# Storing the first of eleven tiles of a row softmax through ScalarE's DMA queue instead of GpSimd's

## The chip, the cores and the metric

The kernel runs on one core of a Trainium2 chip. The core has five engines, each with an instruction stream of its own. Four matter here: VectorE (DVE in the profile), ScalarE (ACT), GpSimd (POOL) and SyncE (SP). Three of them issue transfers: SP all loads, POOL and ACT the stores. The transfers of each issuer form one queue (in the profile's tables q1 is SP's, q0 is POOL's and q10 is ACT's), and all queues are worked off by the same 16 DMA engines. The metric is device time in microseconds (us). The kernel before takes 317.07 us, the median of three runs that lie between 317.07 and 317.11 us.

## What is computed

A softmax over the last axis of a float32 array of 32 x 512 x 1024, with a temperature of 0.5:

```python
scaled = x / temperature
shifted = scaled - np.max(scaled, axis=-1, keepdims=True)
exp_x = np.exp(shifted)
return exp_x / np.sum(exp_x, axis=-1, keepdims=True)
```

That is 16,384 rows of 1024 elements: 67.11 MB are read and 67.11 MB written.

## The kernel before

The rows are cut into eleven tiles (`PASSES`): the first ten hold 12 rows on each of the 128 partitions (6144 KB a tile), the last holds 8 (4096 KB). A tile is worked on in place, in groups of rows: tile 0 in three groups of 4, tiles 1 to 9 in two groups of 6, tile 10 in two groups of 4. There are 23 groups. In what follows, L0 to L10 are the loads of the tiles and S0 to S10 their stores.

Four buffers hold tiles (`BUFS = 4`). A tile is loaded into a buffer by SP (line 60), and the load of tile i+4 waits until the store of tile i has landed, since it takes that buffer. The first four loads are issued at once.

For each group DVE takes the maximum of each row (line 69) and scales it to a bias (line 72); ACT computes the exponentials row by row, with their sum (line 78); DVE takes the reciprocals of the sums (line 90) and multiplies, either all rows in one instruction (line 93, tiles in `WHOLE`) or row by row (line 96). After a tile's last group it is stored (line 108).

The order is written out by hand. For a group g the program emits maximum(g) and exponential(g), and then divide(g-1) and, where g-1 ends a tile, store(g-1) and the load of a further tile. From tile 9 on (`ALONE`), a tile's first group is emitted after the divide and store of the group before it. Each engine runs its own part in that order. So a store issued by ACT stands in ACT's stream behind the exponentials of the group after the tile: S0, if issued by ACT, comes behind the 12 exponentials of tile 0 and the 6 of tile 1's first group, and ahead of the 6 of tile 1's second group.

S0 to S5 are issued by POOL, S6 to S10 by ACT (`BY_POOL = 6`). Ahead of S0, POOL copies one column of tile 2 into a small tile named `seen` (line 106): POOL's stream waits there until L2 has landed. The multiplication of tile 2's first group waits for that copy too, because it overwrites what the copy reads.

Of the kernel before, what the change touches and what calls it, by code (L numbers as in the profile page):

```python
# [1 line left out]

# [4 lines left out]

PASSES = [[4, 4, 4]] + [[6, 6]] * 9 + [[4, 4]]  # L10
BUFS = 4

WHOLE = (2, 3, 4, 6, 8)


BY_POOL = 6

ALONE = 9


@with_exitstack
def kernel(
    ctx: ExitStack,
    tc: tile.TileContext,
    x: bass.AP,
    temperature: bass.AP,
    out: bass.AP,
):
    nc = tc.nc
    f32 = mybir.dt.float32  # L30
    scale = 1.0 / float(temperature)
    extreme = mybir.AluOpType.max if scale > 0 else mybir.AluOpType.min

    P = 128
    xf = x.flatten_outer_dims()
    of = out.flatten_outer_dims()
    n, d = xf.shape
    rows = [sum(ks) for ks in PASSES]
    assert sum(rows) * P == n

    data = ctx.enter_context(tc.tile_pool(name="data", bufs=BUFS))
    stats = ctx.enter_context(tc.tile_pool(name="stats", bufs=4))


    groups = []
    for i, ks in enumerate(PASSES):
        for j, k in enumerate(ks):
            groups.append((i, sum(ks[:j]), k))

    def dram(t, i):  # L50
        block = t[P * sum(rows[:i]) : P * sum(rows[: i + 1]), :]
        return block.rearrange("(p k) d -> p k d", p=P, k=rows[i])

    tiles, small = [], []

    def load():
        i = len(tiles)
        if i < len(PASSES):
            xt = data.tile([P, rows[i], d], f32, name="xt")
            nc.sync.dma_start(out=xt, in_=dram(xf, i))  # L60
            tiles.append(xt)

    def maximum(g):
        i, a, k = groups[g]
        top, bias, sums, recip = (
            stats.tile([P, k], f32, name=name) for name in ("top", "bias", "sums", "recip")
        )
        small.append((bias, sums, recip))
        nc.vector.tensor_reduce(  # L69
            out=top, in_=tiles[i][:, a : a + k, :], axis=mybir.AxisListType.X, op=extreme  # L70
        )
        nc.vector.tensor_scalar_mul(bias, in0=top, scalar1=-scale)  # L72

    def exponential(g):
        i, a, k = groups[g]
        bias, sums, _ = small[g]
        for b in range(k):
            nc.scalar.activation(  # L78
                tiles[i][:, a + b, :],
                tiles[i][:, a + b, :],  # L80
                mybir.ActivationFunctionType.Exp,
                bias=bias[:, b : b + 1],
                scale=scale,
                accum_out=sums[:, b : b + 1],
            )

    def divide(g):
        i, a, k = groups[g]
        _, sums, recip = small[g]
        nc.vector.reciprocal(recip, sums)  # L90
        if i in WHOLE:
            xt = tiles[i][:, a : a + k, :]
            nc.vector.tensor_mul(xt, xt, recip.unsqueeze(2).to_broadcast([P, k, d]))  # L93
            return
        for b in range(k):
            nc.vector.tensor_scalar_mul(  # L96
                tiles[i][:, a + b, :], in0=tiles[i][:, a + b, :], scalar1=recip[:, b : b + 1]
            )

    def store(g):  # L100
        i, a, k = groups[g]
        if a + k == rows[i]:
            if i == 0:


                nc.gpsimd.tensor_copy(stats.tile([P, 1], f32, name="seen"), tiles[2][:, 0, 0:1])  # L106
            queue = nc.gpsimd if i < BY_POOL else nc.scalar
            queue.dma_start(out=dram(of, i), in_=tiles[i])  # L108
            load()

    with tc.manual_schedule():
        for _ in range(BUFS):
            load()
        for g in range(len(groups) + 1):

            alone = g < len(groups) and groups[g][0] >= ALONE and groups[g][1] == 0
            if g > 0 and alone:
                divide(g - 1)  # L120
                store(g - 1)
            if g < len(groups):
                maximum(g)
                exponential(g)
            if g > 0 and not alone:
                divide(g - 1)
                store(g - 1)


# [1 line left out]
_INS = ['x', 'temperature']  # L131
_OUTS = [((32, 512, 1024), 'float32')]

_NUMBERS = {'temperature': 0.5}


# [26 lines left out]
```

## Time and profile before

The profiled execution has a span of 315.8 us from its first to its last instruction; the runs' median is 317.07 us, 1.3 us more.

| | us |
|---|---|
| median of the runs | 317.07 |
| span of the profiled execution | 315.8 |
| DVE busy | 256.9 (81%) |
| ACT busy | 148.3 (47%) |
| POOL busy | 3.7 (1%) |

The DMA engines move 134.24 MB in the span, a mean of 425 GB/s. The trace gives for each transfer its issue and the time to its landing. Worked out as issue plus time to landing:

| tile | load issued | landed | store issued (by) | landed |
|---|---|---|---|---|
| 0 | 0.74 | 18.2 | 47.89 (POOL) | 77.1 |
| 4 | 77.20 | 110.9 | 153.74 (POOL) | 190.3 |
| 5 | 103.10 | 139.7 | 179.94 (POOL) | 221.1 |
| 6 | 132.31 | 168.7 | 211.22 (ACT) | 246.5 |
| 7 | 161.31 | 197.7 | 239.51 (ACT) | 272.5 |
| 8 | 190.44 | 228.5 | 259.97 (ACT) | 290.7 |
| 9 | 221.25 | 257.5 | 284.63 (ACT) | 305.2 |
| 10 | 246.68 | 281.6 | 301.35 (ACT) | 314.9 |

S1, S2 and S3 are issued by POOL at 69.47, 96.49 and 124.95 us and land at 103.1, 132.2 and 161.2 us.

In the page's table of slices each digit is the busy share of a fortieth of the span, in tenths; 9 is 90% or more. In a timeline row the columns are the start, the duration, the engine (ACTq, POOLq, SPq: the sequencer, which issues and waits), the line, the operation, what it writes and reads, the count and, in brackets, the idle time before it with what ended that.

### The profile page before, as it was taken

To read this page: it belongs to the slowest core of one execution; us is meant where nothing else is said; L and a number is where in the kernel's file an instruction comes from. 1 tells how busy PE (TensorE), PEld (TensorE's weight loads), DVE (VectorE), ACT (ScalarE), POOL (GpSimd) and SP (SyncE) were. 2 spreads that over 40 slices of the span, in tenths; PEclk is the share of its full clock that TensorE was granted. 3 is DMA by queue.
4 is the path that set the end of the run, shared out by engine and by line. 5 is a ranking of instruction groups with operands and counts; after the bars stand their busy time and mean duration, and the time that the engine had idled before them with its cause. 6 is when DMAs were issued, how large, how long until landed. Compare 5 with 4: busy or idle time off the path is not lost.

```text
span 315.8 us, 525 instructions
## 1 busy us (share of the span) xinstructions
DVE 256.9 (81%) x147; ACT 148.3 (47%) x257; POOL 3.7 (1%) x11
## 2 busy tenths in 40 slices
DVE  0069999999999899979976994999199999969710
ACT  0029636775461807344471744074416802953700
POOL 0000001000000000000000000000000000000000
DMA  8999999999999999999999999999999999999996
GB/s 305 473 417 423 461 411 399 399 468 430 400 479 417 417 461 411 430 467 405 442 448 399 455 442 405 467 424 417 461 417 430 455 401 463 411 452 411 455 411 270
DMA packets 3171, 134.24 MB, mean 425 GB/s; under 512 B 352, under 2 KB 352, under 8 KB 352
## 3 DMA queue, kind: packets, MB, share of 16 engines
q1 hardware_dynamic: 1584, 67.11, 49.7%
q0 software_dynamic: 864, 37.75, 27.6%
q10 hardware_dynamic: 720, 29.36, 21.5%
q14 instruction: 3, 0.02, 0.0%
HBM read 67.11 MB, written 67.11 MB: 425 GB/s over the span
## 4 chain that ended last, share of the span: by engine, by line
DMA 47%; DVE 28%; ACT 11%; issue 9%; DVEq 0%; SPq 0%; POOLq 0%
DMA xt<-in_x_dram 25%; DMA out_dram<-xt 22%; DVE top L69 16%; ACT xt L78 11%; DVE xt L96 8%; DVE xt L93 2%; DVE bias L72 0%; DVE recip L90 0%; DVEq L158 0%; SPq L60 0%; POOLq L108 0%
## 5 line engine op out<-in xcount | busy, mean ns | idle before, releaser
L78 ACT ACTIVATE xt<-xt,bias 128x1024 f32<-128x1024 f32 x128 | 145.2, 1135 | 131.7 <-DVE recip L90 70.6
L69 DVE TENSOR_REDUCE top<-xt 128x6 f32<-128x6144 f32 (+1 forms) x23 | 139.9, 6083 | 37.8 <-DMA xt<-in_x_dram 37.8
L93 DVE TENSOR_TENSOR xt<-xt,recip 128x6144 f32<-128x6144 f32 x10 | 65.6, 6558 | 0.4
L96 DVE TENSOR_SCALAR xt<-xt,recip 128x1024 f32<-128x1024 f32 x68 | 46.2, 749 | 0.5
L78 ACT ACTIVATION_READ_ACCUMULATOR xt<-xt,bias 128x1 f32 x128 | 23.9, 187 | 0.0
L78 ACT ACT_TABLE_LOAD x1 | 1.3, 1283 | 18.3 <-DMA xt<-in_x_dram 18.3
L90 DVE RECIPROCAL recip<-sums 128x6 f32<-128x6 f32 (+1 forms) x23 | 4.2, 182 | 5.0 <-ACT xt L78 5.0
L108 POOL DMA_DIRECT2D out_dram<-xt x6 | 3.3, 554 | 129.6 <-ACT xt L78 82.7
L72 DVE TENSOR_SCALAR bias<-top 128x6 f32<-128x6 f32 (+1 forms) x23 | 3.9, 171 | 0.8
L106 POOL COPY seen<-xt 128x1 f32<-128x1 f32 x1 | 0.2, 185 | 46.9 <-DMA xt<-in_x_dram 46.9
L144 POOL MEMSET const-uint8-127<- 128x1 uint8 x1 | 0.1, 103 | 0.0
L144 POOL MEMSET const-bfloat16-1.0<- 128x1 bf16 x1 | 0.1, 102 | 0.0
L144 POOL MEMSET const-float32-0.0<- 128x1 f32 x1 | 0.1, 99 | 0.2 <-issue 0.2
L144 POOL MEMSET const-float32-1.0<- 128x1 f32 x1 | 0.1, 98 | 0.0
## 6 DMA issues: line engine op xcount, KB each, us to landing
xt<-in_x_dram SPq DMA_DIRECT2D x10, 6144.0 KB, 36.4
out_dram<-xt POOLq DMA_DIRECT2D x6, 6144.0 KB, 35.9
out_dram<-xt ACTq DMA_DIRECT2D x4, 6144.0 KB, 31.9
xt<-in_x_dram SPq DMA_DIRECT2D x1, 4096.0 KB, 34.9
out_dram<-xt ACTq DMA_DIRECT2D x1, 4096.0 KB, 13.5
```

The source lines that it names most:

```text
L69: nc.vector.tensor_reduce(out=top, in_=tiles[i][:, a : a + k, :], axis=mybir.AxisListType.X, op=extreme)
L72: nc.vector.tensor_scalar_mul(bias, in0=top, scalar1=-scale)
L78: nc.scalar.activation(tiles[i][:, a + b, :], tiles[i][:, a + b, :], mybir.ActivationFunctionType.Exp, bias=bias[:, b : b + 1], scale=scal ...
L90: nc.vector.reciprocal(recip, sums)
L93: nc.vector.tensor_mul(xt, xt, recip.unsqueeze(2).to_broadcast([P, k, d]))
L96: nc.vector.tensor_scalar_mul(tiles[i][:, a + b, :], in0=tiles[i][:, a + b, :], scalar1=recip[:, b : b + 1])
L106: nc.gpsimd.tensor_copy(stats.tile([P, 1], f32, name="seen"), tiles[2][:, 0, 0:1])
L108: queue.dma_start(out=dram(of, i), in_=tiles[i])
L144: nc = _bacc.Bacc("TRN2", target_bir_lowering=False, num_devices=1)
```

## The change

S0 is issued by ACT. S1 to S5 stay with POOL and S6 to S10 with ACT. The copy into `seen` stays in POOL's stream, now ahead of S1. Nothing else in the program is different: the arithmetic, the tiles, the buffers and the order of the groups are the same.

```diff
                 nc.gpsimd.tensor_copy(stats.tile([P, 1], f32, name="seen"), tiles[2][:, 0, 0:1])
-            queue = nc.gpsimd if i < BY_POOL else nc.scalar
+            queue = nc.gpsimd if 0 < i < BY_POOL else nc.scalar
             queue.dma_start(out=dram(of, i), in_=tiles[i])
             load()
```

In the built program ACT's stream gains one transfer, which waits for DVE alone, and POOL's loses one. SP's loads stand in the same order; the load of tile 4 still waits for S0's landing.

## The prediction

> **What bounds the kernel now.** I read the slices of the whole span first, then the DMA view in stretches, then the issues of the stores one by one, and last the chain of waits for the tail.
>
> ```profile
> span 315.8 us, 525 instructions
> DMA  8999999999999999999999999999999999999996
> HBM read 67.11 MB, written 67.11 MB: 425 GB/s over the span
> ```
>
> The DMA engines are busy in every slice but the first and the last. The DMA view of four stretches (20 to 49, 49 to 60, 60 to 280 and 305 to 316 us):
>
> ```profile
> DMA packets 288, 12.58 MB, mean 434 GB/s; under 512 B 32, under 2 KB 32, under 8 KB 32
> ...
> DMA packets 88, 4.33 MB, mean 393 GB/s; under 512 B 0, under 2 KB 0, under 8 KB 0
> ...
> DMA packets 2235, 95.45 MB, mean 434 GB/s; under 512 B 248, under 2 KB 248, under 8 KB 248
> ...
> DMA packets 118, 3.34 MB, mean 304 GB/s; under 512 B 16, under 2 KB 16, under 8 KB 16
> ```
>
> Loads alone (20 to 49) go at 434 GB/s. So does the stretch from 60 to 280, in which loads mix with stores of POOL and then of ACT. So 434 GB/s is what this core's engines give, whatever the mix and whoever issued. At that rate 134.24 MB take 309.3 us; 6.5 us of the span are something else:
> - start: the stretch 0 to 20 moves 7.86 MB, which is 18.1 us of work: 1.9 us lost;
> - 49 to 60, where S0 joins L3: 4.33 MB are 10.0 us of work in 11: **1.0 us lost**, the only dip between the ends;
> - 305 to 316: 3.34 MB are 7.7 us of work in 10.8: 3.1 us lost, of which 0.9 lie behind the last landing (301.35 + 13.5 = 314.85) and 2.2 are engines that finish unevenly.
>
> Together 6.0, with 0.5 of rounding at the edges of the stretches. So the kernel is bound by DMA throughput; the compute matters only where it would leave the queues empty. The timeline around S0 and around ACT's first store of now (S6):
>
> ```profile
> 47.31 0.18 POOL L106 COPY seen<-xt 128x1 f32<-128x1 f32 x1 [46.86 <-DMA xt<-in_x_dram]
> 47.35 6.55 DVE L69 TENSOR_REDUCE top<-xt 128x6 f32<-128x6144 f32 x1
> 47.89 0.67 POOL L108 DMA_DIRECT2D out_dram<-xt  x1 [0.40 <-DVE xt L96]
> ...
> 50.29 1.13 ACT L78 ACTIVATE xt<-xt,bias 128x1024 f32<-128x1024 f32 x1
> ...
> 54.20 1.15 ACT L78 ACTIVATE xt<-xt,bias 128x1024 f32<-128x1024 f32 x1 [2.68 <-DVE recip L90]
> ...
> 69.47 0.53 POOL L108 DMA_DIRECT2D out_dram<-xt  x1 [20.91 <-DVE xt L96]
> ...
> 210.21 1.13 ACT L78 ACTIVATE xt<-xt,bias 128x1024 f32<-128x1024 f32 x1
> 211.22 0.97 ACTq L108 DMA_DIRECT2D out_dram<-xt  x1
> ...
> 301.35 0.34 ACTq L108 DMA_DIRECT2D out_dram<-xt  x1
> ```
>
> To be seen here: the copy into `seen` holds S0 back by nothing, since the multiplications of tile 0 end with the start of the maximum at 47.35; POOL has 20.91 us of idle time ahead of S1; and ACT idles 2.68 us ahead of its work at 54.20.
>
> **The change part by part.**
>
> *S0 leaves POOL.* Removed: one issue of 0.67 us on an engine that is 1% busy: 0 us, hidden by POOL's 20.91 us of idle time. S1 waits for DVE until 69.17 in any case, and the copy ahead of it is over at 47.5: S1 to S5 keep their times.
>
> *S0 stands in ACT's stream.* ACT runs in order, so S0 waits for the exponentials of tile 1's first group. S6 was issued 1.01 us after the start of the last exponential ahead of it (210.21 to 211.22); the same behind 50.29 gives 51.30. S0 is issued **3.4 us later** than at 47.89. Its wait for DVE (47.4) is long over. The issue takes between 0.34 us (ACT's later ones, 301.35) and 0.97 us (its first, S6); S0 is now the first, so I take 0.97, to 52.3. What is queued behind it is the exponential of 54.20, which waits for DVE's bias anyway: 1.9 us to spare, cost 0. Without that cover, ACT would be late by 0.97 us at most, and DVE's reciprocal behind it by as much. S6's issue becomes a later one and shrinks by 0.6 us; its cover is the 6.40 us that ACT idles behind it: 0.
>
> *S0 and S1 lie on two queues.* Before, S1 stood behind S0 on POOL's queue. Now they can run side by side from about 70 us. The nearest row is S5, whose last 10 us ran beside S6 from ACT's queue: 41.2 us to landing, against 36.6 for S4, so 4.6 longer. L8, in flight at the same time, took 38.1 against the 36.4 of L6 and L7. For S0 that is an upper bound, since L3 loses nothing by S0's later start and gets out of the way sooner. S0 would land between 77.1 + 3.4 = 80.5 and 80.5 + 4.6 = 85.1. I take 81, nearest to the lower end: S1's first turns come only when S0 has a quarter left. L4 waits for this landing, is issued 3.4 to 8 us later and lands by about 3.5 us later (114 for 110.9). DVE, which waits 1.67 us for L4 now, waits about 5.
>
> The Trainium skill's page "DMA: Bandwidth & Descriptors", section "Queues, rings and completion order", speaks against the change here: each DMA engine takes turns between the queue rows that have work, a packet at a time, so a second row for stores takes turns from whatever is in flight. By the rule alone, what S0 has left when S1 begins (some 8 us: 80.5 less 72) would take twice as long and L4 be issued near 88.5 instead of 77.2; carried whole to the tail that would be some 10 us. By the row of S5 it is 8 us at most, and the next step says why I carry none of it.
>
> *Where that stall goes.* Nothing is lost as long as some queue has work. Late next is L4 by 3.5 us; but the engines' turns that L4 doesn't take are taken by S1, which lands some 4 us sooner than 103.1, and L5 is issued then, behind L4. From there a load is always waiting: before, L5 is issued at 103.1 and L4 lands at 110.9, and each pair after that overlaps by 7 us. A later L4 makes these overlaps longer. The stores, ahead by as much, run dry once for some microseconds around S6, and there the loads catch up. Work done in another order: 0 us.
>
> *The tail.* The chain from L8's landing (228.5) through DVE and ACT to S10's issue (301.35) has no DMA wait in it. S10 lands 13.5 us after its issue, since S9 lands only at 305.2 and 4.19 MB take 9.7 us at 434 GB/s. L0, with 14.5 us of data, landed 17.5 after its issue, so a lone S10 would need 9.7 + 3.0 = 12.7: the chain has **0.8 us of slack**. I take L8 as not later than now, since S5 and S6 overlap less; cost 0.
>
> *The dip of 1.0 us at S0.* The trace of before shows that it comes with the first store; it doesn't show whether with the first write at all, with the first use of POOL's queue, or with that queue joining loads. When ACT's queue is first used (S6, 212 to 222) the rate is 452 GB/s, no dip. With the first write, it stays, at S0; with POOL's first use, it moves to S1. Bounds: -1.0 (it goes) to +1.0 (one at S0 and another at S1). I take 0, which two of the readings give.
>
> Sum: 0 + 0 + 0 + 0 + 0. Span 315.8, and with the 1.3 us around it **317.1 us**, the median of the runs. The uneven finish of the engines (2.2 us) can shift by some tenths either way, so the forecast's own range is 316.5 to 317.7.
>
> **The rivals.**
> - *The dip goes* (28%). For it: ACT's first use showed none, and when POOL's queue is now first used, at 69.5, L3 may have landed, so no load is there to be held up. Against: the first packets of the program are slow too, so a first use may cost in itself. 317.1 - 1.0 = **316.1**.
> - *The dip doubles* (13%). For it: two queues each have their first use amid full engines. Against: S6. 317.1 + 1.0 = **318.1**.
> - *L4's lateness reaches the tail* (12%). The mechanism: L5 to L8 stand behind L4 on one queue, 29 us apart (110.9, 139.7, 168.7, 197.7), so 3.5 us pass whole from each to the next; if the stores don't run dry before L8, it lands at 232.0 and the tail's chain starts that late. It decides from 0.8 us on. 317.1 + 3.5 - 0.8 = **319.8**; with L4 late by 8 it would be 324. Against: stores that are ahead have to run dry, as a load can't be late and the engines full without that.
> - *The change doesn't do what it says*: S0 might not start later or on another queue. The built order excludes it: the transfer stands behind 18 exponentials on ACT. No share.
>
> **How the numbers follow.** What a measurement can tell from no change is about 0.2%, 0.6 us. Forecast 47%, all within that; faster 28% from the first rival; slower 25% from the second and third. The likeliest gives 317.1. The range reaches to 315.9 (the dip gone, the finish a little more even) and to 318.3 (a second dip): it leaves out the 12% of the late tail and little else.
>
> **What would show it.** ACT's issue of S0 at about 51.3; the next exponential still near 54.2; S0's landing near 81, L4's near 114, S1's near 99; L8's not later than 228.5; S10's issue before 301.4. The DMA view from 49 to 60, and around S1 from 69 to 80, tells where the dip is: near 393 GB/s in one of them is the forecast, in neither the first rival, in both the second. The prediction is wrong if the dip is bound to loads and POOL's queue together, or if the DMA slices show a gap that is not there now.

## The result, and the profile after

The changed kernel takes 319.32 us (median of 7, 318.66 to 321.12) against 317.11 us for the kernel before in the same comparison (median of 7, 317.02 to 318.92). The ratio is 1.0065, 95% interval 1.0044 to 1.0086: slower by 2.2 us, where no change was forecast. In a second comparison the medians were 321.16 (8 executions) and 318.40 us (19), the ratio 1.0089 (1.0053 to 1.0124). Single executions of the kernel before scatter, and more than these first seven show: of 139 in the later comparisons 80 lie under 318 us and 52 between 318.5 and 320.5, while none of the 15 of the changed kernel lies under 318.6.

The page of the changed kernel, in the lines that were shown of the kernel before:

```profile
span 317.8 us, 524 instructions
DMA  8999999999999999999999999999999999999984
HBM read 67.11 MB, written 67.11 MB: 422 GB/s over the span
```

The digits differ only at the end: 9 and 6 before, 8 and 4 now. The same bytes have moved with full engines all the way, and the last two slices are emptier. The DMA view from 49 to 60 us and from 69 to 80 us:

```profile
DMA packets 86, 4.23 MB, mean 384 GB/s; under 512 B 0, under 2 KB 0, under 8 KB 0
...
DMA packets 121, 4.87 MB, mean 442 GB/s; under 512 B 22, under 2 KB 22, under 8 KB 22
```

The dip is still at the first store, now by ACT's queue (384 GB/s, before 393), and there is none where POOL's queue is first used (442). So it goes with the first write, whichever of the two queues brings it. 4.23 MB are 9.7 us of work at 434 GB/s, so it costs 1.3 us now, 0.3 more.

The timeline around S0:

```profile
46.91 1.13 ACT L78 ACTIVATE xt<-xt,bias 128x1024 f32<-128x1024 f32 x1
47.37 6.55 DVE L69 TENSOR_REDUCE top<-xt 128x6 f32<-128x6144 f32 x1
47.48 0.37 ACTq L108 DMA_DIRECT2D out_dram<-xt  x1
48.05 1.13 ACT L78 ACTIVATE xt<-xt,bias 128x1024 f32<-128x1024 f32 x1
...
50.31 1.13 ACT L78 ACTIVATE xt<-xt,bias 128x1024 f32<-128x1024 f32 x1
```

S0 is issued at 47.48, as soon as DVE is done with tile 0, while ACT's engine still has three of the six exponentials to run that stand ahead of it. So the sequencer, which issues, did not wait for them. S0 is thus 0.4 us earlier than before, not 3.4 us later.

From the issues and their times to landing, the changed kernel has S0 from 47.48 to 83.5 (before 47.89 to 77.1), S1 from 69.48 to 98.0 (103.1), L4 from 83.59 to 114.3 (110.9), L5 landed at 139.7 (139.7), L6 at 168.8 (168.7), L7 at 198.3 (197.7), **L8 at 230.9 (228.5)**, S10 from 303.75 to 316.5 (301.35 to 314.9).

Why does S0 take 36.0 us? Each of the 16 DMA engines ends its share of a transfer with a packet of 4 bytes; the view counts these as "under 512 B", and a transfer has landed when all 16 are in. The DMA view of the kernel before from 75.9 to 77 us, where S0 ends:

```profile
DMA packets 32, 0.79 MB, mean 715 GB/s; under 512 B 16, under 2 KB 16, under 8 KB 16
```

And of the changed kernel from 79.5 to 81, 81 to 82.5 and 82.5 to 84 us:

```profile
DMA packets 31, 0.79 MB, mean 524 GB/s; under 512 B 15, under 2 KB 15, under 8 KB 15
...
DMA packets 16, 0.75 MB, mean 497 GB/s; under 512 B 0, under 2 KB 0, under 8 KB 0
...
DMA packets 16, 0.74 MB, mean 492 GB/s; under 512 B 1, under 2 KB 1, under 8 KB 1
```

Before, all 16 engines end S0 within 1.1 us. Now 15 have ended by 81, then comes a stretch without any, and the sixteenth ends by 84 (at 83.16 in the packet records). L4 is issued at 83.59; by then fifteen of the engines had been done with S0 for over 2 us. The Trainium skill's page "DMA: Bandwidth & Descriptors", section "Why a DMA increments its semaphore by 16 and not by 1", says that only the full count of 16 means that the data has landed; the 83.16 and the 83.59 here agree.

The same engine-by-engine reading of the end, kernel before from 312.8 to 314.6 us, then the changed kernel from 314.3 to 316.3 and from 314.55 to 316.3:

```profile
DMA packets 17, 0.03 MB, mean 18 GB/s; under 512 B 16, under 2 KB 16, under 8 KB 16
```

```profile
DMA packets 17, 0.03 MB, mean 16 GB/s; under 512 B 16, under 2 KB 16, under 8 KB 16
...
DMA packets 2, 0.03 MB, mean 19 GB/s; under 512 B 1, under 2 KB 1, under 8 KB 1
```

In the changed kernel the last 1.7 us belong to one engine: one data packet (0.03 MB) and its closing one. Fifteen were done by 314.55, which is where the kernel before ended altogether.

In what follows, the *lag* is the time of the sixteenth closing packet of a transfer less the median of the sixteen, read from the packet records of the trace (these times lie 0.3 to 0.4 us ahead of the landings). In the kernel before it is 1.3 us at L8 and at S10; in the changed kernel 3.6 and 1.8. The median engine's L8 ends at 226.8 and at 226.9 us: the typical engine has lost nothing there.

At S9 the lag is 1.3 us in the kernel before and 2.9 in the changed one. The DMA view of the kernel before from 303.1 to 304.9 us, where all 16 engines end S9, then of the changed kernel from 304.8 to 306.6, where one still has to, and the changed kernel's issue of S10:

```profile
DMA packets 42, 0.85 MB, mean 473 GB/s; under 512 B 16, under 2 KB 16, under 8 KB 16
...
DMA packets 17, 0.52 MB, mean 291 GB/s; under 512 B 1, under 2 KB 1, under 8 KB 1
```

```profile
303.75 0.34 ACTq L108 DMA_DIRECT2D out_dram<-xt  x1
```

By the packet records the last engine ends S9 at 304.84 us in the kernel before and at 306.52 in the changed one, 1.68 later, and the median one at 303.59 and 303.66. In both kernels, and in every other profiled run of this document, the last engine ends S10 9.7 us after its S9, which is S10's 4.19 MB at 434 GB/s. So the engine that ends the kernel goes from S9 to S10 without a pause. The median engine of the changed kernel does pause for S10's late issue (its first packets start at 304.6), yet ends at 314.42, 1.8 us ahead of the last.

### The profile page after: what moved, and what is told of

Its sections match the earlier page's. It is cut to its first block, busy times and chain, and to the rows that moved or that the text cites. A ratio compares the mean times of both kernels' runs of the same rounds, so it can differ in the third digit from the quotient of the medians.

```text
span 317.8 us, 524 instructions
## 1 busy us (share of the span) xinstructions
DVE 256.8 (81%) x147; ACT 148.3 (47%) x257; POOL 3.2 (1%) x10
## 4 chain that ended last, share of the span: by engine, by line
DMA 50%; DVE 25%; ACT 12%; issue 8%; DVEq 0%; SPq 0%; POOLq 0%
DMA xt<-in_x_dram 28%; DMA out_dram<-xt 23%; DVE top L69 15%; ACT xt L78 12%; DVE xt L96 5%; DVE xt L93 4%; DVE bias L72 0%; DVE recip L90 0%; DVEq L158 0%; SPq L60 0%; POOLq L108 0%
```

## The experiments

The theories, in the order in which they came: (1) the chain from L8's landing to S10's issue, which starts late, sets the end. (2) S0 on ACT's queue costs in itself; in the form (2b), it is L4's lateness that costs. (3) Turns of the DMA engines are lost in mid-run. (4) With the early stores on two queues beside the loads, the slowest engine gives its turns away and falls behind. (5) POOL's queue makes packets slow. (6) An engine that is late once falls back further by itself.

The results that compare queues (four more runs stand with their numbers below); times are medians with the lowest and highest, the ratio is to the kernel before on the same chip with its 95% interval, and the lags are those of the one profiled execution of each. In the edits, a `-` line with `0 < i`, and the edit to `BY_POOL = 7`, belong to the changed kernel; the others, where the text says no more, to the kernel before.

| kernel | median us | lowest, highest | ratio (95%) | lag L8, S10 (us) |
|---|---|---|---|---|
| changed | 319.32 | 318.66, 321.12 | 1.0065 (1.0044, 1.0086) | 3.6, 1.8 |
| changed, again | 321.16 | 319.84, 322.00 | 1.0089 (1.0053, 1.0124) | 4.7, 1.4 |
| before, again | 317.55 | 317.16, 320.83 | 1.0002 (0.9966, 1.0039) | 3.3, 2.0 |
| S1 to S6 by POOL | 319.08 | 318.03, 320.60 | 1.0041 (1.0016, 1.0067) | 4.7, 3.4 |
| S0 by ACT, rest by POOL | 319.69 | 318.13, 320.91 | 1.0035 (1.0008, 1.0063) | 3.9, 3.3 |
| S1 alone by ACT | 320.02 | 318.45, 321.91 | 1.0051 (1.0020, 1.0083) | 3.2, 2.9 |
| S0 and S1 by ACT | 319.87 | 318.43, 322.57 | 1.0060 (1.0028, 1.0091) | 2.7, 1.4 |
| S2 alone by ACT | 318.97 | 317.93, 320.32 | 1.0018 (0.9991, 1.0044) | 3.1, 1.9 |
| S0 by POOL, rest by ACT | 318.23 | 317.46, 320.89 | 1.0014 (0.9981, 1.0047) | 4.7, 3.7 |
| all by ACT | 317.90 | 317.37, 318.81 | 1.0000 (0.9980, 1.0021) | 1.4, 1.3 |
| all by POOL | 317.92 | 317.45, 319.96 | 1.0001 (0.9974, 1.0028) | 0.5, 0.8 |
| all by POOL, again | 319.01 | 317.68, 319.58 | 1.0018 (0.9993, 1.0043) | 0.7, 0.7 |
| S0 later, by POOL | 318.42 | 317.57, 320.17 | 1.0006 (0.9975, 1.0037) | 2.8, 1.5 |
| changed, no last division | 320.68 | 320.34, 321.59 | 1.0099 (1.0079, 1.0118) | 6.9, 4.5 |
| before, no last division | 317.73 | 316.86, 319.82 | 1.0016 (0.9994, 1.0038) | 3.0, 2.9 |

The profiled execution of the repeat of the kernel before took 319.29 us, with a lag of 3.3 us at L8 against 1.3 in the first one, whose span was 1.8 us shorter. In these two, the lag goes with the time within one kernel too.

### Is it the tail, and is it the crossing at S5 and S6?

S1 to S6 by POOL, so that the later change of queue falls between S6 and S7:

```diff
-BY_POOL = 6
+BY_POOL = 7
```

> S0 by ACT as in the changed kernel, but S1 to S6 by POOL and only S7 to S10 by ACT. Theory 1 (S5 on POOL's queue and S6 on ACT's run side by side with the loads, so that L8 gets a third of the turns and lands at 230.9, and the tail's chain starts late): S5 and S6 follow each other on one queue, L8 lands by 228.5, S10 is issued by 301.5 and the time falls to 317.0 to 317.6 us. Theory 2 (L4's lateness of 3.4 us, or S0 on ACT's queue as such, costs the time): L8 stays near 231, the time near 319.3. Theory 3 (the dip at the first store, grown from 1.0 to 1.3 us, and other lost DMA turns): 319.3, wherever L8 lands.

Measured: 319.08 us, lowest 318.03, ratio 1.0041. L8's last engine ends at 229.8, 0.8 sooner than in the changed kernel, but L10's at 285.7 (284.8), and most of the loss stays. Theory 1 loses its first support, the change of queue at S5 and S6. The late chain itself is still there: L8 lands at 230.1 in place of the 228.5 expected, and S10 is issued at 303.06.

All stores by ACT:

```diff
-            queue = nc.gpsimd if 0 < i < BY_POOL else nc.scalar
+            queue = nc.scalar
```

> All eleven stores by ACT, so the stores form one queue throughout. Theory 1: no stretch with three queues, L8 lands by 228, the time 317.0 to 317.6 us. Theory 2 in the form that an early store on ACT's queue costs in itself: 319 or more. In the form that L4's lateness costs: S0 has no S1 beside it here, lands near 77 and L4 near 111, so 317 too; the landing of L4 then tells the two apart from the run with S6 by POOL.

Measured: 317.90 us, ratio 1.0000. S0 is issued by ACT at 48.01 and lands after 30.0 us. All 16 engines end S0 between 76 and 78 us, and the last one ends S10 at 314.8. The DMA view of this kernel from 76 to 78 us, then from 314.2 to 315:

```profile
DMA packets 34, 0.88 MB, mean 442 GB/s; under 512 B 16, under 2 KB 16, under 8 KB 16
...
DMA packets 1, 0.00 MB, mean 0 GB/s; under 512 B 1, under 2 KB 1, under 8 KB 1
```

An early store on ACT's queue costs nothing measurable where the other stores are on it too (interval 0.9980 to 1.0021). Theory 2 falls.

The division of tile 10 left out, in the changed kernel and in the kernel before (tile 10 is stored as plain exponentials):

```diff
         _, sums, recip = small[g]
+        if i == len(PASSES) - 1:
+            return
         nc.vector.reciprocal(recip, sums)
```

> The changed kernel without the division of tile 10 (its rows are stored as plain exponentials). S10 is then issued behind ACT's last exponential, about 3 us sooner (300.7 for 303.75). Theory 1 (the end waits for the chain from L8 to S10): the time falls by the 1 to 2 us in which the DMA engines ran dry ahead of S10, to 317.3 to 318.2 us. Theory 3 (turns lost earlier): falls by less than 0.3 us.

> The kernel before without the division of tile 10. S9's transfer ends behind S10's issue there, so the engines don't run dry: all theories 316.7 to 317.1 us, no change. A fall of over 1 us would say that the chain set the end there too.

Measured: 320.68 and 317.73 us. The changed kernel did not fall, though S10 was issued sooner. Its timeline there, and its DMA view from 314.6 to 318.3 us:

```profile
302.13 0.34 ACTq L110 DMA_DIRECT2D out_dram<-xt  x1
```

```profile
DMA packets 5, 0.10 MB, mean 27 GB/s; under 512 B 2, under 2 KB 2, under 8 KB 2
```

S10 is issued 1.6 us sooner than at 303.75 and yet the end comes later: after 314.6, two engines of the sixteen are still at work, with three data packets between them, and the last ends at 318.2, 4.5 us behind the median one. What sets the end is the backlog of the last engine; the chain through DVE and ACT does not. Theory 1 falls, by this and by the last engine's unbroken work from S9 to S10 above. Theory 3 predicted the absence of a gain, but no turns are missing for the typical engine: it ends S10 at 313.7 here and at 313.3 in the kernel before. (Of the kernel before, 316.7 to 317.1 us had been expected; 317.73 is above that, and the ratio, 1.0016, is not told from no change.)

### Is it S0, or the two queues?

> The kernel before with S1 alone moved to ACT's queue: S0 stays with POOL. Theory 4: S0 and S1 lie on two store queues beside L3 just as in the changed kernel, so S0 lands past 81, L4 is issued that late, and the time is 318.3 to 320 us. Theory 2 (S0 on ACT's queue, or its start 0.4 us sooner, costs): S0 is untouched, 317.1 to 317.5 us.

```diff
-            queue = nc.gpsimd if i < BY_POOL else nc.scalar
+            queue = nc.gpsimd if i < BY_POOL and i != 1 else nc.scalar
```

Measured: 320.02 us, ratio 1.0051. S0 is where it was (POOL, issued at 48.00) and lands at 80.7, L4 at 114.0. Its 16 engines end S0 together (lag 0.4), yet the last one is 3.2 us behind at L8. S1's queue alone makes a loss of the same size. Theory 2 is refuted a second time. Theory 4 is met on the time, but not in its mechanism: S0 lands late here with no engine behind the others.

```diff
-            queue = nc.gpsimd if 0 < i < BY_POOL else nc.scalar
+            queue = nc.gpsimd if 1 < i < BY_POOL else nc.scalar
```

> S0 and S1 by ACT, S2 to S5 by POOL, S6 to S10 by ACT. Theory 4: S1 stands behind S0, so S0 lands near 77.5 and L4 near 111 as in the kernel before; the crossing to a second store queue moves to S1 and S2, with L4 in flight. The early part costs nothing; the crossing there can cost as much as at S0, so the time lies between 317.3 and 319.5 us, and L5, which waits for S1, lands 2 us late if it does. Theory 2 (an early store on ACT's queue costs in itself): 319 or more with S0 landing past 82.

Measured: 319.87 us, ratio 1.0060; S0's last engine ends at 77.4. The early part is as in the kernel before, and the change of queue between S1 and S2 costs as much as the one between S0 and S1. (The profiled execution, 318.43 us, is the fastest of its twelve.)

```diff
-            queue = nc.gpsimd if 0 < i < BY_POOL else nc.scalar
+            queue = nc.gpsimd
```

> All eleven stores by POOL: one queue of stores throughout, as with all by ACT. Theory 4: no crossing at all, S0 lands near 77, L8's landing spreads by little over 1 us between the engines, time 317.0 to 318 us. Theory 5 (POOL's queue makes single packets slow, as its ring is shared): slow packets as in the changed kernel and 318.5 or more.

> All stores by POOL again, for comparison on the same chip: 317.4 to 318.5 us, lag at S10 near 1 us.

Measured: 317.92 and, in a later comparison, 319.01 us; neither ratio tells them from the kernel before (1.0001 and 1.0018). In the profiled executions S10's lag is 0.8 and 0.7 us. Theory 5 falls. In the second set six of 12 executions lie at 319.3 to 319.6 and the profiled one is the fastest (317.68), so one queue is no full protection.

```diff
-            queue = nc.gpsimd if 0 < i < BY_POOL else nc.scalar
+            queue = nc.sync if i == 0 else nc.gpsimd if i < BY_POOL else nc.scalar
```

> S0 issued by SP, behind L3 on the loads' own queue; S1 to S5 by POOL, S6 to S10 by ACT. Theory 4 (new, after the first four runs: when a second queue of stores joins while the slowest of the 16 DMA engines still has packets of L3 and S0, that engine's turns go to S1, so the transfers that others wait for land with it, 3 us behind the rest; the slowest engine then ends last): here S0 shares turns with S1 alone, L3 is finished before S0 starts, so S0 lands near 78, and the time is 316.8 to 317.7 us. Theory 2 (an S0 on a hardware queue beside S1 on POOL's costs in itself): 319. The dip at the first store: no load is in flight when S0 starts, so if the dip holds up loads only, it is gone and the time is near 316.3.

Measured: 322.81 and 322.98 us in two executions, 327.92 to 330.74 in four. The ratio, 1.0148 (1.0085 to 1.0212), is that of the two; the profile (329.15) is one of the four. Every theory missed this. S0 lands at 84.20 and S1 at 93.24, but SP, whose wait ahead of them ends with S1's landing, issues its next two loads, L4 and L5, only then, one right behind the other. SP's issues there, and the DMA view from 84 to 96 us and from 140 to 170:

```profile
93.29 0.80 SPq L60 DMA_DIRECT2D xt<-in_x_dram  x2
```

```profile
DMA packets 83, 3.29 MB, mean 274 GB/s; under 512 B 16, under 2 KB 16, under 8 KB 16
...
DMA packets 239, 11.30 MB, mean 377 GB/s; under 512 B 9, under 2 KB 9, under 8 KB 9
```

From 84 to 96 us the engines run short of work (274 GB/s; before 414 in this stretch), and from 140 to 170 they are busy but move 377 GB/s (before 424). So this run did not test the queues of the stores alone: L4 waited for S1 as well. Why the packets are slow later is not explained here.

### One change of queue, or two; and does lateness matter?

> S0 by POOL, all others by ACT: one crossing between two queues of stores, early, none at S5 and S6. Theory 4: S0 lands past 80 and one of the 16 engines falls behind; if the early crossing alone suffices, 318.5 to 320 us; if it takes the second crossing at S5 and S6 to stretch the lag, 317.4 to 318.2 us.

> S0 by ACT as in the changed kernel, all others by POOL: again one early crossing and none later. Theory 4: like the run with S0 by POOL and the rest by ACT, 318.5 to 320 us if the early crossing suffices, 317.4 to 318.2 us if it takes both. Theory 2 (ACT's queue for S0): 319 here and 317.2 in the mirrored run.

The first edit is one of the kernel before, the second one of the changed kernel:

```diff
-BY_POOL = 6
+BY_POOL = 1
```

```diff
-            queue = nc.gpsimd if 0 < i < BY_POOL else nc.scalar
+            queue = nc.gpsimd if 0 < i else nc.scalar
```

Measured: 318.23 us (1.0014, not told from the kernel before; three of 12 under 318) and 319.69 us (1.0035, none of 12 under 318). With S0 by ACT, the early change of queue alone suffices. With S0 by POOL the verdict is open: its profiled execution (320.49 us) has S0's last engine at 80.9 and a lag of 4.7 us at L8, but others are as fast as the kernel before.

> The kernel before with S2 alone moved to ACT: crossings at S1 and S2 and at S2 and S3, with loads always in flight, S0 and L4 untouched. Theory 4: any further crossing gives the last engine's turns away, 318 to 320 us. Theory 2b (only L4's lateness counts): 317.1 to 317.9 us.

```diff
-            queue = nc.gpsimd if i < BY_POOL else nc.scalar
+            queue = nc.gpsimd if i < BY_POOL and i != 2 else nc.scalar
```

Measured: 318.97 us, ratio 1.0018 (0.9991 to 1.0044): not told from no change, one of 12 under 318. By the ratio a later pair of changes costs less than an early one, if anything. But of the kernel before 21 of 35 executions on that chip lie under 318, so this run and the one with S0 by POOL (three of 12) may carry part of the loss.

```diff
-                nc.gpsimd.tensor_copy(..., tiles[2][:, 0, 0:1])
+                nc.gpsimd.tensor_copy(..., small[3][1][:, 5:6])
```

> The kernel before, S0 to S5 by POOL; POOL's copy ahead of S0 reads ACT's last sum of tile 1's first group in place of tile 2, so S0 is issued near 52 and lands near 80.5, L4 near 114, with one queue of stores until S6. Theory 4 (two queues of stores beside the loads early): no early crossing, 317.0 to 317.9 us. Theory 2b (it is L4's lateness of 3 us that costs, whatever its cause): 318.5 to 320 us.

Measured: 318.42 us, ratio 1.0006. The run did not do what it was made for: S0, issued 4.7 us later, took 25.3 us instead of 29.2 (L3 landed at 68.8 in place of 73.2), and its last engine ended at 77.5. L4 was not late. Theory 2b is not tested by it.

### Does a late engine fall back by itself?

All stores by POOL, and SP stores 17 partitions of one row of tile 0 a second time:

```diff
             queue.dma_start(out=dram(of, i), in_=tiles[i])
+            if i == 0:
+                nc.sync.dma_start(out=dram(of, 10)[0:17, 0:1, :], in_=tiles[0][0:17, 0:1, :])
```

> All stores by POOL (317.9 us with no further change), and SP stores 17 partitions of one row of tile 0 a second time, into the rows of tile 10, which S10 overwrites later. 17 can't be shared out among 16 engines, so 69.6 KB go through few engines or one: 2.6 us of work at 27 GB/s for one engine (434 GB/s divided by 16), near 62 us, with one queue of stores throughout. Theory 6 (an engine that is late falls back further by itself): the last engine's packets get slow as in the changed kernel, 3 to 5 us in all, and the time rises by more than 2.6 us, to 320.5 or more. Theory 4 (it takes a second queue of stores): slow packets stay near 1 us and the time rises by at most the inserted work, to 318.5 to 320.3 us.

Measured: 330.94 us, ratio 1.0395. It does not answer the question: L4 had to wait for the added store and was issued at 93.75. The cause is instructive, though. The 17 packets of 4 KB stood behind L3 on one engine, and took turns with S0's and S1's packets of 48 KB. By the packet records eleven of them start about 1.97 us apart, from 72.56 to 92.39, a packet of 48 KB (1.8 us) between each two. That agrees with the Trainium skill's page "DMA: Bandwidth & Descriptors", section "Queues, rings and completion order", by which an engine drains a whole packet from one queue before it turns to the next. As in the run by SP, L4 and L5 then start together (93.75 and 94.20), and the engines are slow again later; the DMA view from 140 to 170 us:

```profile
DMA packets 251, 11.55 MB, mean 385 GB/s; under 512 B 16, under 2 KB 16, under 8 KB 16
```

```diff
             queue.dma_start(out=dram(of, i), in_=tiles[i])
+            if i == 1:
+                queue.dma_start(
+                    out=dram(of, 9)[0:1].rearrange("p k d -> p (k d)")[:, 0:12281],
+                    in_=tiles[1][0:1].rearrange("p k d -> p (k d)")[:, 0:12281],
+                )
```

The first of the next two has all stores by POOL, the second is the kernel before with the same addition.

> All stores by POOL, and behind S1 one store of 12,281 elements of tile 1 from one partition into tile 9's rows (S9 overwrites them later): one packet of 1.8 us on one DMA engine. Theory 6 (a late engine falls back further by itself): the lag of the last engine grows from about 3 us at L5 to over 4 at L10, slow packets 2.5 us or more in all, time 319.5 to 321 us. Theory 4 (it takes a second queue of stores): the lag stays at 2 to 3 us from L5 to S10, slow packets 1 to 1.7 us, time at most 1.8 us over the kernel with one queue: 318 to 319.7 us.

> The kernel before (S0 to S5 by POOL, the rest by ACT) with the same packet added behind S1. Theories 4 and 6 alike: the lag is stretched where S5 and S6 lie on two queues, L8's last engine is 3.3 us or more behind the median one, and nearly all executions lie at 319 to 321 us, as the slower ones of the kernel before do now. If the lag does not matter: 317.2 to 317.6 in over half of them, as before.

Measured: 318.34 us (318.20 to 318.96) and 318.20 us (317.77 to 319.90), ratios 1.0001 and 0.9993. The added packet left no engine late: L8's lag is 0.9 and 1.6 us. Theory 6 stays untested. (Of the kernel before, 11 of 29 executions on that chip lay over 318.9; with the added store, 2 of 12, in line with a small lag.)

> The changed kernel again: 318.7 to 321 us, its last engine 1.8 us or more behind the median one at S10, single packets slow by 2.5 us or more in all.

> The kernel before again: 317.0 to 318 us in most executions and up to 320 in some; in an execution near 317 the last engine ends about 1.2 us behind the median one, and slow packets come to less than 2 us; in one near 319 they come to 3 us or more.

Measured: 321.16 and 317.55 us. The second is as expected for most of its executions (up to 320.83 in others); the first lies just above its range of 318.7 to 321, and its lag at S10 is 1.4 us where 1.8 or more was expected. In the second profile of the changed kernel S0's last engine ends at 83.4 again, 3.2 us behind the median one, and L8's at 231.9. There the lag does not shrink on the way: it is 3.2 to 4.0 us at L5, L6 and L7, where the first profile has 1.3 to 1.8.

### What is shown, and what is open

Shown: the change is slower by 0.4% to 1.2% (the two intervals together); the end is set by the last DMA engine out of 16, which works without a pause from S9 through S10; neither ACT's queue, nor S0 alone, nor the tail's chain is the cause; stores S0 to S2 on two queues bring the loss in five kernels (the changed one, S1 to S6 by POOL, S0 by ACT with the rest by POOL, S1 alone, S0 and S1), two more such kernels (S2 alone, S0 by POOL with the rest by ACT) are undecided, and one queue of stores never brings it measurably in three comparisons.

Open: why that engine falls behind. The packets of 49,152 bytes take 1.815 us in nearly all records. What single ones over 1.85 us take beyond that, from 58 us on and over all engines, sums to 1.7 us in the kernel before, 1.3 and 0.9 with one queue, and to 2.5, 4.6, 3.9, 5.0 and 3.1 us in the five slower kernels. But it is 3.0 in the repeat with one queue (317.68 us) and 9.4 and 6.6 in the two runs with the added packet, which lose nothing, so this sum alone does not make the loss. Whether the lag makes packets slow or slow packets make the lag, the runs don't tell. Theory 2b is open too: L4 lands at 112.3 to 114.7 us in the five slower kernels, at 110.9 in the kernel before and at 110.1 to 111.0 with one queue, and no run here made L4 late with its stores on one queue and nothing else changed. The Trainium skill's page "DMA: Bandwidth & Descriptors" lists, in "Latency and other measured facts", two DMA engines that are usually slower than the others; the records used here don't name the engine, so no run here shows whether it is one of those.

## Why the prediction was wrong, by its own steps

- *What bounds the kernel* (DMA throughput, 434 GB/s for any mix): held. The full slices are as full as before.
- *S0 leaves POOL, and what is behind it on ACT is not held up*: held; S1 is issued at 69.48 and the next exponential starts at 54.22.
- *S0 is issued 3.4 us later*: wrong. It was read from S6, which starts 1.01 us after ACT's last exponential; but S6 was released by DVE, whose multiplication, in the row below, ends at 204.58 + 6.56 = 211.14, 0.08 us ahead of S6. The error changed no sign: S0 landed later all the same.

```profile
204.58 6.56 DVE L93 TENSOR_TENSOR xt<-xt,recip 128x6144 f32<-128x6144 f32 x1
```

- *S0 lands at 81, L4 at 114, S1 near 99*: 83.5, 114.3 and 98.0. S0 lies within the bounds given (80.5 to 85.1) by luck: S0 was issued sooner, not later, and landed late by sharing with S1 and by its last engine.
- *Where that stall goes*: L4's 3.4 us were made up by L5 (139.7 in both), as argued; in the second profile not whole (L5 141.9, L7 200.7, against 139.7 and 197.7 before). The stores did not run dry around S6, as the step had it: S6 was issued at 211.82, well ahead of S5's landing at 223.6. **The step that failed** is its last sentence, "Work done in another order: 0 us". It treats the sixteen engines as one server. For the median engine it is right (L8 at 226.8 and 226.9). But a transfer lands with its last engine, and so does the kernel.
- *The uneven finish can shift by some tenths*: this is the term that was mis-sized. The rows for it were there and were held constant. (2.2 us were booked as uneven finish; by the packet records the sixteen engines of the kernel before end S10 on the mean 1.1 us ahead of their last, and the rest of the 2.2 is landing and the edge of the window.) The last engine's lateness moved the end by 1.7 us (314.5 to 316.2), and by up to 3.7 in the runs. Why that engine falls behind stays open.
- *The dip*: stays at the first write, as forecast; 0.3 us larger.
- *The tail, 0.8 us of slack, and the third rival*: L8 did land 2.4 us late, and 2.4 - 0.8 = 1.6 matches S10's landing (1.7 later). The match misled: with S10 issued 1.6 us sooner, the end did not come sooner. The rival had the sign and the place, not the cause. The slack was larger than 0.8 too: a lone S10 was put at 12.7 us from L0's row, but S10's packets start 0.9 us after its issue, and the last engine of the kernel before ends S9 only at 304.84, so, by an estimate from these rows, an issue at 303.9, which is 2.6 us later, would have cost nothing. What the rival asked for, L4's lateness passed on whole from load to load, is not in the first profile either: L5 to L7 were on time or within 0.6 us.

## What to carry to other kernels

Where full DMA engines bound a kernel, "the same bytes in another order" is free only for the average engine: look at the closing packets of a transfer one by one, since whoever waits for it waits for the sixteenth. Keep a stream that others wait for on one queue, or change its queue late; here one store moved to a second queue near the start cost 0.4% to 1.2%, and the change of queue at S6 cost nothing measurable. A time that matches a chain's lateness is no proof that the chain sets the end: shorten the chain and see.

## What had not been expected of the hardware

- A transfer in ACT's stream is issued when the semaphores it names are set, ahead of three exponentials that stand before it (47.48 us, with ACT busy until 51.4).
- The first write of the program slowed the loads in flight by 1.0 to 1.3 us of work, from POOL's queue and from ACT's; the first use of a second queue didn't (442 GB/s).
- In both runs in which L4 and L5 were issued together near 93.5 us, the engines moved 377 and 385 GB/s while busy between 140 and 170 us.
- In every profiled run the last of the 16 engines ended S10 9.7 us after S9, without a pause, so its backlog at S9 set the end.
- 17 packets of 4 KB on one engine beside large ones held a load back from 77.2 to 93.75 us.
